# Modulation passes of a diffusion step's first layer: other places among the linear attention's VectorE work

## The chip, the cores and the metric

The kernel runs on one core of a Trainium2 chip. The metric is the device time of one launch in microseconds (us). The core's engines run side by side, each with its own queue of instructions in a fixed order: TensorE (PE in the profile, its weight loads PEld), VectorE (DVE), ScalarE (ACT), GpSimd (POOL) and SyncE (SP), whose queue issues nearly all DMA loads here. An instruction that waits holds up everything behind it on its engine.

## The reference, cut to what matters

A step of a diffusion backbone with two layers, over 512 latent and 128 context tokens of width 1024. Each layer has a mixer and a gated convolution FFN; both are modulated by vectors that come from a conditioning vector:

```python
def modulation(cvec, w, bias):
    mod = (jax.nn.silu(cvec) @ w + bias).reshape(-1, 1, 6 * D_MODEL)
    return jnp.split(mod, 6, axis=-1)      # sh1, sc1, g1, sh2, sc2, g2
...
hp = rms_norm(xp, norm_mix_g[i]) * (1.0 + sc1p) + sh1p
...
xp = xp + g1p * op
xp = xp + g2p * conv_ffn(rms_norm(xp, norm_ffn_g[i]) * (1.0 + sc2p) + sh2p, *ffn)
```

The same is done for the latent tokens with their own conditioning vector. The first layer's mixer is neighbourhood attention (8 heads) beside a bidirectional gated linear attention (4 heads, chunks, decay from log_sigmoid gates, forward and backward). The linear attention's gates are `log_sigmoid(lr @ w2 + b2) / 16`, summed along the tokens; its scores weigh q and k with exponentials of differences of these sums, its states carry k and v from tile to tile.

## The kernel before

All 640 tokens lie along the free axis, in two halves of 320; features lie on the partitions. Matmuls are done in three passes on a high and a low part (line 153): the weights are split into wh (ScalarE, line 111) and wl (VectorE or GpSimd, line 112).

**Modulation beside the first layer.** `modulations` is a generator. It makes three vectors (second gate of the mixer and the FFN's shift and scale) on VectorE, without TensorE: for each of 3 vectors, 8 feature tiles and 2 halves it loads a tile `wa` of 128x512 (256 KB, line 313, SP's queue, three buffers) and runs two scalar_tensor_tensor passes over it (line 316), one for the latent and one for the context vector, each with an accumulator read. That is one step; there are 48. Behind each vector's 16 steps come four small additions (lines 320 and 321).

**Order of the work.** The program's order is a priority: a planner gives each engine, at compile time, the ready instruction that stands first, by its own estimate of times. So an instruction may run well ahead of or behind its place in the program. `tc.issue_after(ins)` ties the instructions traced in its block to a place behind `ins` where they are on the same engine; instructions of other engines, and loads, aren't tied.

**The first layer.** `layer0` multiplies keys and queries of the linear attention, makes the low-rank input `lr` of the gates (weights `lrs`, lines 651 to 669), takes one step of the modulation, and then walks the linear attention: four gates (VectorE's `gmin`, line 730, ScalarE's exponentials and logarithms), four running sums `cum` (lines 743 and 745), then the pieces of `ORDER`: scores of m = 0 (`a0`), states of m = 0 (`s0`), scores of m = 1 (`a1`), output of m = 0 (`o0`), the first query projection (`q0`), `s1`, `o1`. m counts pairs of heads. Scores are made in six levels of growing block width and two off-diagonal ones: four subtractions on VectorE (`ea`, `eb`, lines 840 to 843), two exponentials on ScalarE, a product on GpSimd (line 846) and one on VectorE (line 847), small matmuls `lev` or `off` on TensorE, and a mask on VectorE (line 865). The tiles of this part share 16 buffers of one tag, `c`.

**Fill.** `Fill` holds generators of independent TensorE work (the products for v, the output gate rg, the attention's values: `tm` in lines 592 to 594 and `mm` in line 153) and hands out some of it at each call `fill.some(n)` along the chain: behind each gate, each sum, each level, in the states and in the outputs. `aside` holds the modulation. Its second argument `m` says how many modulation steps are taken at this call: SLEV = 2 at each of six levels, SOFF = 4 behind them, and 99, that is all that are left, ahead of the states.

Of the kernel before, what the change touches and what calls it, by code (L numbers as in the profile page):

```python
# [12 lines left out]
ALU = mybir.AluOpType  # L13
# [8 lines left out]
HN = NT // 2  # L22
# [8 lines left out]
def kernel(ctx: ExitStack, tc: tile.TileContext, a: dict, o: dict):  # L31
    nc = tc.nc
# [43 lines left out]
    def halves(t):  # L76
        return t[:, 0:NT].rearrange("p (h n) -> p h n", h=2)
# [29 lines left out]
    b2 = const("b2", [P, 2, 2])  # L107
# [131 lines left out]
    class Fill:  # L239


        def __init__(self):
            self.queue, self.aside, self.owed, self.after = [], [], 0.0, None

        def add(self, gen):
            self.queue.append(gen)
# [1 line left out]
        def first(self, gen):  # L248
            self.queue.insert(0, gen)

        def some(self, n, m=0):
            while m and self.aside:
                m -= 1
                if next(self.aside[0], self) is self:
                    self.aside.pop(0)
            self.owed += n
            n = int(self.owed)
            self.owed -= n
            while n and self.queue:
                with tc.high_priority(offset=0):  # L260
                    end = next(self.queue[0], self) is self
                if end:
                    self.queue.pop(0)
                else:
                    n -= 1

        def until(self, gen):

            while gen in self.queue:
                self.some(1)  # L270

        def all(self):
            while self.queue:
                self.some(1)


    mod = {}
# [353 lines left out]
    def layer0(H, raws):  # L631
        fill = Fill()
# [29 lines left out]
        ps = PS("lr")  # L662
# [52 lines left out]
        nxt = qk(0)  # L715
        barrier.clear()
        fill.aside.append(side)


        gscan = N("gscan")  # L720
# [4 lines left out]
        for m, d in keys:  # L725
            ps = PS("gate")
            for h in range(2):
                nc.tensor.matmul(ps[:, h, 0:HN], w2[:, d, 128 * m:128 * m + 128], lr[0:64, h * HN:(h + 1) * HN], start=True, stop=True)
            mn, ab = C("gmin"), C("gabs")
            nc.vector.tensor_scalar(halves(mn), ps[:, :, 0:HN], b2[:, d, m:m + 1], 0.0, ALU.add, ALU.min)  # L730
            nc.scalar.activation(halves(ab), ps[:, :, 0:HN], AF.Abs, bias=b2[:, d, m:m + 1])
            mins[m, d], logs[m, d] = mn, ab
            last = nc.scalar.activation(ab, ab, AF.Exp, scale=-1.0)
            fill.some(RG1)
# [3 lines left out]
        for key in keys:  # L738
            m, d = key
            nc.vector.tensor_tensor(mins[key], mins[key], logs[key], ALU.subtract)  # L740
            c = C("cum")
            if d == 0:
                nc.vector.tensor_tensor_scan(c, gscan, mins[key], 0.0, ALU.mult, ALU.add)
            else:
                nc.vector.tensor_tensor_scan(rev(c), gscan, rev(mins[key]), 0.0, ALU.mult, ALU.add)
            cum[key] = c
            fill.some(RG2)


        with tc.issue_after(last.ins):  # L750
            S, OT, att = {}, {}, {}

            def piece(kind, m):
                nonlocal last
                if kind == "a":
                    att.update(gla_scores(m, kg[m], qg[m], cum[m, 0], cum[m, 1], fill))
                elif kind == "s":
                    fill.until(g_vg)
                    fill.some(0, 99)
                    gla_states(m, kg[m], cum[m, 0], cum[m, 1], vg, S, fill)  # L760
                elif kind == "o":
                    last = gla_out(m, qg[m], cum[m, 0], cum[m, 1], vg, att, S, OT, fill)
                else:
                    fill.first(nxt)

            for p in ORDER:
                piece(p[0], int(p[1]))
        fill.until(g_va)
        with tc.issue_after(last):
            for t in rg:  # L770
# [52 lines left out]
    def rev(t):  # L823
        return t[:, ::-1]
# [7 lines left out]
    def gla_scores(m, k, q, F, G, fill):  # L832
        def level(h):

            ea, eb = C("ea"), C("eb")
            v = lambda t: t[:, 0:NT].rearrange("p (n s u) -> p n s u", s=2, u=h)
            n = NT // (2 * h)
            fm_ = v(F)[:, :, 0, h - 1:h].to_broadcast([P, n, h])
            gm_ = v(G)[:, :, 1, 0:1].to_broadcast([P, n, h])
            nc.vector.tensor_tensor(v(ea)[:, :, 0, :], fm_, v(F)[:, :, 0, :], ALU.subtract)  # L840
            nc.vector.tensor_tensor(v(ea)[:, :, 1, :], gm_, v(G)[:, :, 1, :], ALU.subtract)
            nc.vector.tensor_tensor(v(eb)[:, :, 0, :], v(G)[:, :, 0, :], gm_, ALU.subtract)
            nc.vector.tensor_tensor(v(eb)[:, :, 1, :], v(F)[:, :, 1, :], fm_, ALU.subtract)
            expo(ea[:, 0:NT], ea[:, 0:NT])
            expo(eb[:, 0:NT], eb[:, 0:NT])
            nc.gpsimd.tensor_tensor(ea[:, 0:NT], ea[:, 0:NT], k[:, 0:NT], ALU.mult)
            nc.vector.tensor_tensor(eb[:, 0:NT], eb[:, 0:NT], q[:, 0:NT], ALU.mult)  # L847
            return ea, eb

        accs = C("acc")  # L850
        acc, tmp = accs[:, 0:320], accs[:, 320:640]
        for li, h in enumerate(LEVELS):
            A, B = (k, q) if h == 0 else level(h)
            ps = PS("lev")
            for t in range(5):
                for e in range(2):
                    pe = slice(64 * e, 64 * e + 64)
                    for j in range(4):
                        s = slice(128 * t + 32 * j, 128 * t + 32 * j + 32)
                        nc.tensor.matmul(ps[32 * j:32 * j + 32, e, 32 * t:32 * t + 32], A[pe, s], B[pe, s], start=True, stop=True)  # L860
            for e in range(2):
                pv = ps[:, e, 0:160].rearrange("p (t i) -> p t i", i=32)
                mk = mask32[:, li:li + 1, :].to_broadcast([P, 5, 32])
                w = acc if li == 0 else tmp
                nc.vector.tensor_tensor(w[:, 160 * e:160 * e + 160].rearrange("p (t i) -> p t i", i=32), pv, mk, ALU.mult)
            if li:
                nc.gpsimd.tensor_tensor(acc[:, 0:320], acc[:, 0:320], tmp[:, 0:320], ALU.add)
            fill.some(RLEV, SLEV)
        A32, B32 = level(32)
        A64, B64 = level(64)  # L870
        fill.some(ROFF, SOFF)
        big, small = PS("off"), PS("offx")
        res = {}
        blocks = [(e, slice(64 * e, 64 * e + 64), t, big[:, e, 128 * t:128 * t + 128] if t < 4 else small[:, e, 0:128])
                  for e in range(2) for t in range(5)]
        for width in (32, 64):
            for e, pe, t, dst in blocks:
                if width == 32:
                    for j in range(4):
                        b = j // 2  # L880
                        s = slice(128 * t + 32 * j, 128 * t + 32 * j + 32)
                        nc.tensor.matmul(dst[32 * j:32 * j + 32, 64 * b:64 * b + 64], A32[pe, s],
                                         B32[pe, 128 * t + 64 * b:128 * t + 64 * b + 64], start=True, stop=True)
                    continue
                for b in range(2):
                    nc.tensor.matmul(dst[64 * b:64 * b + 64, 64 - 64 * b:128 - 64 * b],
                                     A64[pe, 128 * t + 64 * b:128 * t + 64 * b + 64],
                                     B64[pe, 128 * t + 64 - 64 * b:128 * t + 128 - 64 * b], start=True, stop=True)
        for e in range(2):
            x = C("att")  # L890
            nc.scalar.copy(x[:, 0:512], big[:, e, :])
            nc.scalar.copy(x[:, 512:640], small[:, e, 0:128])
            for j in range(4):
                pj = slice(32 * j, 32 * j + 32)
                nc.vector.tensor_copy(
                    x[pj, 0:NT].rearrange("p (t i) -> p t i", i=128)[:, :, 32 * j:32 * j + 32],
                    acc[pj, 160 * e:160 * e + 160].rearrange("p (t i) -> p t i", i=32),
                )
            res[m, e] = x
        return res  # L900

    def gla_states(m, k, F, G, vg, S, fill):
# [13 lines left out]
        for d in range(2):  # L916
# [13 lines left out]
            nc.sync.dma_start(s[:, 0, :], a["gla_s"][d, m])  # L930
            for i, t in enumerate(tiles[0:3]):
                nc.vector.scalar_tensor_tensor(s[:, i + 1, :], s[:, i, :], dec[d][:, t:t + 1], ds[:, 128 * i:128 * i + 128], ALU.mult, ALU.add)
            nc.vector.tensor_copy(s[:, 4, :], ds[:, 384:512])
            nc.gpsimd.dma_start(o["gla"][d, m], s[:, 4, :])
            S[m, d] = s
            fill.some(RST)
# [536 lines left out]
RLEV = 7  # L1473
ROFF = 12
RST = 8
ROUT = 6
SLEV = 2
SOFF = 4
ORDER = ("a0", "s0", "a1", "o0", "q0", "s1", "o1")
WPOOL = {'mix0': 2}  # L1480
NV = (False, True)
# [130 lines left out]
```

## Time and profile before

| | us |
|---|---|
| median of 3 runs | 1732.13 |
| lowest and highest run | 1729.12, 1733.19 |
| profiled execution, time | 1732.08 |
| profiled execution, span from first to last instruction | 1730.3 |
| VectorE busy over the span | 1280.7 (74%) |
| TensorE matmul busy over the span | 1640.0 (95%) |

The profile is of one execution. A row's busy time counts an instruction from its start to its end, with waits for a port inside it. Stretches are given in us from the start of the span.

### The profile page before, as it was taken

How to read it: one execution, taken by the hardware profiler on the slowest of the kernel's cores; microseconds unless marked ns; L12 is line 12 of the kernel's file. 1: busy time of each engine (PE TensorE's matmuls, PEld its weight loads, DVE VectorE, ACT ScalarE, POOL GpSimd, SP SyncE). 2: the span in 40 equal slices, each digit the busy share in tenths (PEclk: the TensorE clock that was granted, in tenths of full speed). 3: DMA queues.
4: the chain of work that ended last, by engine and by line, in shares of the span. 5: the costliest groups of instructions: out<-in, count | busy, mean ns of one | idle time of the engine just before them, and what ended most of it. 6: DMA issues, size and time to landing. Idle time of an engine off the chain costs nothing.

```text
span 1730.3 us, 33463 instructions
## 1 busy us (share of the span) xinstructions
PE 1640.0 (95%) x13142; PEld 1565.2 (90%) x13142; DVE 1280.7 (74%) x2877; ACT 720.9 (42%) x1599; POOL 206.5 (12%) x475
## 2 busy tenths in 40 slices
PE   7978798989999999999999999899999999999997
PEld 6867787878999999999998888789999999999997
DVE  5899955775899989996656987996776644663664
ACT  4443255453533313322335566665453322331342
POOL 2134441210200000000003310100100000000001
PEclk8988889999999999999998999999999999999998
DMA  8624323322255455444232200120222222222222
GB/s 317 204 86 133 108 90 97 101 88 92 81 165 164 152 165 183 151 149 128 70 122 87 68 20 13 42 63 20 80 66 82 74 74 73 74 69 91 72 66 71
DMA packets 68014, 175.22 MB, mean 101 GB/s; under 512 B 7920, under 2 KB 9744, under 8 KB 66832
## 3 DMA queue, kind: packets, MB, share of 16 engines
q1 hardware_dynamic: 67024, 171.48, 30.7%
q8 instruction: 103, 1.69, 0.4%
q0 software_dynamic: 832, 1.60, 0.3%
q14 instruction: 55, 0.45, 0.1%
HBM read 165.71 MB, written 7.34 MB: 100 GB/s over the span
## 4 chain that ended last, share of the span: by engine, by line
PE 78%; DVE 15%; DMA 3%; ACT 2%; issue 2%; SPq 0%; POOL 0%; ACTq 0%; DVEq 0%; POOLq 0%
PE mm L153 66%; DVE junk L316 2%; PE gpo L1297 2%; DVE wa L316 2%; PE gpt L1285 1%; DVE wl L112 1%; PE gs L1276 1%; DMA wa<-in_ada_wt_dram 1%; DVE mx L1023 1%; PE gs L1277 1%; PE napo L1089 1%; PE ss L410 1%; DVE eb L847 1%; DMA x<-in_xT_dram 0%; DVE q L613 0%
## 5 line engine op out<-in xcount | busy, mean ns | idle before, releaser
L153 PE MATMUL mm<-hh,wl 128*128 128x320 f32 x2080 | 652.6, 316 | 5.3 <-DVE x L488 1.9
L153 PE MATMUL mm<-hl,wh 128*128 128x320 f32 x2080 | 648.3, 312 | 0.6 <-DVE hl L456 0.6
L153 PE MATMUL mm<-hh,wh 128*128 128x320 f32 x2080 | 641.9, 312 | 0.0
L111 ACT CAST wh<-ws 128x512 fp32r<-128x512 f32 x376 | 228.8, 615 | 447.8 <-PE mm L153 420.5
L153 PEld LDWEIGHTS mm<-hh,wl 128*128 128x128 f32 x2080 | 394.5, 190 | 15.8 <-issue 5.5
L153 PEld LDWEIGHTS mm<-hl,wh 128*128 128x128 f32 x2080 | 395.2, 190 | 3.0 <-issue 1.2
L153 PEld LDWEIGHTS mm<-hh,wh 128*128 128x128 f32 x2080 | 393.4, 190 | 0.4
L112 DVE TENSOR_TENSOR wl<-ws,wh 128x512 fp32r<-128x512 f32 x348 | 242.2, 699 | 157.4 <-ACT wh L111 156.7
L153 PE MATMUL mm<-glo,wh 128*128 128x320 f32 x704 | 217.6, 310 | 0.0
L153 PE MATMUL mm<-ghi,wh 128*128 128x320 f32 x704 | 217.3, 310 | 0.0
L153 PE MATMUL mm<-ghi,wl 128*128 128x320 f32 x704 | 216.3, 310 | 0.0
L488 DVE SCALAR_TENSOR_TENSOR x<-mm,mod,x 128x192 f32<-128x192 f32 (+2 forms) x240 | 96.6, 435 | 84.1 <-PE mm L153 83.2
L153 PEld LDWEIGHTS mm<-ghi,wl 128*128 128x128 f32 x704 | 132.0, 188 | 0.9 <-issue 0.9
L153 PEld LDWEIGHTS mm<-glo,wh 128*128 128x128 f32 x704 | 132.6, 188 | 0.0
L153 PEld LDWEIGHTS mm<-ghi,wh 128*128 128x128 f32 x704 | 132.4, 188 | 0.1
L316 DVE SCALAR_TENSOR_TENSOR junk<-wa,sb 128x512 f32<-128x512 f32 x160 | 120.4, 757 | 9.4 <-DMA wa<-in_ada_wt_dram 7.0
L316 DVE SCALAR_TENSOR_TENSOR wa<-wa,sb 128x512 f32<-128x512 f32 x160 | 113.2, 714 | 0.2
L522 POOL MEMSET u<- 128x1 f32 x88 | 8.9, 102 | 767.2 <-DVE gate L515 432.5
L525 ACT COPY u<-mm 128x320 f32<-128x320 f32 x88 | 37.8, 431 | 87.6 <-PE mm L153 83.2
L1029 ACT ACTIVATE gp<-gs,mx,rq 128x640 f32<-128x640 f32 x64 | 56.9, 889 | 36.6 <-DVE mx L1025 27.9
L592 PE MATMUL tm<-wl,hh 128*128 128x256 f32 x200 | 61.3, 312 | 8.3 <-ACT v L601 4.0
L528 ACT COPY u<-mm 128x192 f32<-128x192 f32 x88 | 28.4, 322 | 78.8 <-PE mm L153 78.8
(302 smaller groups left out, 2452.7 us busy)
## 6 DMA issues: line engine op xcount, KB each, us to landing
ws<-in_wu_dram SPq DMA_DIRECT2D x88, 512.0 KB
wa<-in_ada_wt_dram SPq DMA_DIRECT2D x160, 256.0 KB
ws<-in_wd_dram SPq DMA_DIRECT2D x32, 448.0 KB
aw<-in_ada_w_dram SPq DMA_DIRECT2D x8, 1024.0 KB
ws<-in_w_ab_dram SPq DMA_DIRECT2D x16, 512.0 KB
ws<-in_wd_dram SPq DMA_DIRECT2D x16, 512.0 KB
x<-in_xT_dram SPq DMA_DIRECT2D x16, 320.0 KB
ws<-in_w_gqa_dram SPq DMA_DIRECT2D x10, 512.0 KB
```

The source lines that it names most:

```text
L111: nc.scalar.copy(hi, src)
L112: eng.tensor_tensor(lo, src, hi, ALU.subtract)
L153: nc.tensor.matmul(ps, x, y[:, s], start=st, stop=sp_)
L316: nc.vector.scalar_tensor_tensor(w if v else junk, w, 1.0, cs[v, j], ALU.mult, ALU.mult, accum_out=acc[:, k, v, j:j + 1])
L410: nc.tensor.matmul(ps[0:rows, c:c + 2], part[:, t], onesd, start=True, stop=True)
L488: nc.vector.scalar_tensor_tensor(x[:, b:e], ps[:, b - HN * h:e - HN * h], gate[:, v, m:m + 1], old[:, b:e], ALU.mult, ALU.add)
L525: nc.scalar.copy(u[:, 1:321], ps)
L528: nc.scalar.copy(u[:, 321:513], ps[:, 0:192])
L592: nc.tensor.matmul(ps, hh[:, s], wlo, start=(k == 0), stop=False)
L847: nc.vector.tensor_tensor(eb[:, 0:NT], eb[:, 0:NT], q[:, 0:NT], ALU.mult)
L1029: nc.scalar.activation(dst, src, AF.Exp, bias=mx[:, i:i + 1], accum_out=sm[:, i:i + 1], **kw)
L1297: last = nc.tensor.matmul(po[64 * f:64 * f + 64, 0:128], vs[t][:, 64 * kv:64 * kv + 64], mates[f]["x"][:, 128 * t:128 * t + 128], start=(t ...
```

## The change

Modulation steps are no longer the second argument of `some`. A new method `beside` takes steps, each tied behind `anchor`, the VectorE instruction that the chain last set. `some` adds `pace` (PACE = 3.0) to a counter at each call and takes as many steps; `queued` hands out the fill as before. The anchors are gmin, cum, the level's mask and the last copy of a state. Ahead of the states nothing is flushed any more; behind the last piece `beside(999)` would take what is left.

```diff
-        def some(self, n, m=0):
-            while m and self.aside:
-                m -= 1
-                if next(self.aside[0], self) is self:
-                    self.aside.pop(0)
+        def beside(self, n):
+
+            while n and self.aside:
+                n -= 1
+                with ExitStack() as behind:
+                    if self.anchor is not None:
+                        behind.enter_context(tc.issue_after(self.anchor.ins))
+                    if next(self.aside[0], self) is self:
+                        self.aside.pop(0)
+
+        def some(self, n):
+            self.due += self.pace
+            self.beside(int(self.due))
+            self.due -= int(self.due)
+            self.queued(n)
+
+        def queued(self, n):
             self.owed += n
...
         fill.aside.append(side)
+        fill.pace = PACE
...
-            nc.vector.tensor_scalar(halves(mn), ps[:, :, 0:HN], b2[:, d, m:m + 1], 0.0, ALU.add, ALU.min)
+            fill.anchor = nc.vector.tensor_scalar(halves(mn), ps[:, :, 0:HN], b2[:, d, m:m + 1], 0.0, ALU.add, ALU.min)
...
-                nc.vector.tensor_tensor_scan(c, gscan, mins[key], 0.0, ALU.mult, ALU.add)
+                fill.anchor = nc.vector.tensor_tensor_scan(c, gscan, mins[key], 0.0, ALU.mult, ALU.add)
...
-                    fill.some(0, 99)
...
+        fill.beside(999)
         fill.until(g_va)
...
-                nc.vector.tensor_tensor(w[:, 160 * e:160 * e + 160].rearrange("p (t i) -> p t i", i=32), pv, mk, ALU.mult)
+                fill.anchor = nc.vector.tensor_tensor(w[:, 160 * e:160 * e + 160].rearrange("p (t i) -> p t i", i=32), pv, mk, ALU.mult)
...
-            fill.some(RLEV, SLEV)
+            fill.some(RLEV)
...
-        fill.some(ROFF, SOFF)
+        fill.some(ROFF)
...
-            nc.vector.tensor_copy(s[:, 4, :], ds[:, 384:512])
+            fill.anchor = nc.vector.tensor_copy(s[:, 4, :], ds[:, 384:512])
...
-SLEV = 2
-SOFF = 4
+PACE = 3.0
```

The backward running sum (line 745) sets the anchor in the same way, and `until` and `all` call `queued` in place of `some`.

## Rows read from the trace of the kernel before

**Rows 1.** The page's 40 slices: busy tenths of TensorE and VectorE.
```profile
PE   7978798989999999999999999899999999999997
...
DVE  5899955775899989996656987996776644663664
```

**Rows 2.** Busy time by stretch: length, then per engine busy us and instructions, clock, DMA.
```profile
54.00:82.50 28.50, 25.86 (x162) 24.27 (x161) 26.61 (x68) 8.59 (x21) 5.60 (x4) 0.94 0.62 203
82.50:111.40 28.90, 25.86 (x256) 23.58 (x255) 28.01 (x61) 16.25 (x26) 4.11 (x2) 0.94 0.46 153
111.40:164.50 53.10, 38.88 (x708) 36.12 (x707) 53.10 (x104) 18.16 (x36) 26.12 (x16) 0.84 0.29 93
164.50:224.00 59.50, 47.75 (x777) 44.72 (x777) 59.37 (x128) 17.72 (x32) 27.80 (x19) 0.87 0.33 110
224.00:264.00 40.00, 39.37 (x426) 35.54 (x425) 17.75 (x35) 22.96 (x45) 17.34 (x15) 0.93 0.29 96
```

The engines' order is PE, PEld, DVE, ACT, POOL.

**Rows 3.** The same stretches, line 316 on VectorE alone.
```profile
54.00:82.50 28.50, 19.78 (x55) 0.94 0.62 203
82.50:111.40 28.90, 13.84 (x40) 0.94 0.46 153
111.40:164.50 53.10, 20.98 (x45) 0.84 0.29 93
164.50:224.00 59.50, 25.20 (x54) 0.87 0.33 110
```

**Rows 4.** TensorE's waits, 111.4 to 224 us, then 164.5 to 224: sum, times, longest.
```profile
PE lev L860 <- DVE eb L847: 14.2, 6, 5.2
...
PE ds L927 <- ACT kt L922: 2.7, 1, 2.7
...
PE lev L860 <- DVE eb L847: 7.5, 3, 4.9
```

**Rows 5.** VectorE's waits, 54 to 224 us.
```profile
DVE junk L316 <- DMA wa<-in_ada_wt_dram: 1.9, 5, 0.6
```

**Rows 6.** The chain of waits in 70 to 98 us: start, length, what; the longest of four DMA pieces.
```profile
82.01 4.15 DMA wa<-in_ada_wt_dram
```

**Rows 7.** SP's waits, 54 to 224 us.
```profile
SPq L313 <- DVE wa L316: 89.3, 39, 10.4
```

**Rows 8.** Timeline of ScalarE, VectorE and TensorE before the gates: start, length, instruction.
```profile
64.26 0.49 ACT L659 CAST lrs<-lrw 128x128 fp32r<-128x128 f32 x2
...
68.12 0.48 DVE L660 TENSOR_TENSOR lrs<-lrw,lrs 128x128 fp32r<-128x128 f32 x2
...
76.52 0.81 DVE L669 COPY lr<-lr 64x640 f32<-64x640 f32 x1
...
82.52 0.87 DVE L730 TENSOR_SCALAR gmin<-gate,b 128x640 f32<-128x640 f32 x1
...
62.28 0.44 PE L592 MATMUL tm<-wl,hh 128*128 128x256 f32 x1 [2.08 <-DVE wl L112]
...
75.29 0.46 PE L666 MATMUL lr<-hl,lrs 128*128 128x320 f32 x2
...
79.60 2.42 PE L728 MATMUL gate<-lr,w 64*128 64x320 f32 x8
```

**Rows 9.** TensorE busy behind 220 us: line 153, then line 592.
```profile
220.00:264.00 44.00, 15.57 (x92) 13.71 (x93) 0.89 0.28 94
...
220.00:264.00 44.00, 5.57 (x14) 4.20 (x14) 0.89 0.28 94
```

**Rows 10.** VectorE's groups of line 316, 164.5 to 224 us, then 54 to 82.5: busy, mean ns.
```profile
L316 DVE SCALAR_TENSOR_TENSOR junk<-wa,sb 128x512 f32<-128x512 f32 x13 | 13.1, 1021 | 0.0
L316 DVE SCALAR_TENSOR_TENSOR wa<-wa,sb 128x512 f32<-128x512 f32 x14 | 13.1, 938 | 0.0
...
L316 DVE SCALAR_TENSOR_TENSOR junk<-wa,sb 128x512 f32<-128x512 f32 x14 | 11.1, 791 | 3.4 <-DMA sb<-in_crow_dram 2.2 <-DMA wa<-in_ada_wt_dram 1.0
L316 DVE SCALAR_TENSOR_TENSOR wa<-wa,sb 128x512 f32<-128x512 f32 x14 | 9.3, 680 | 0.2
```

More of the change, by code (lines that the diff above doesn't have):

```diff
@@ L243, in __init__ @@
             self.queue, self.aside, self.owed, self.after = [], [], 0.0, None
+            self.pace, self.due, self.anchor = 0, 0.0, None
         def add(self, gen):
@@ L269, in until @@
             while gen in self.queue:
-                self.some(1)
+                self.queued(1)
         def all(self):
             while self.queue:
-                self.some(1)
+                self.queued(1)
     mod = {}
@@ L742, in layer0 @@
             if d == 0:
-                nc.vector.tensor_tensor_scan(c, gscan, mins[key], 0.0, ALU.mult, ALU.add)
+                fill.anchor = nc.vector.tensor_tensor_scan(c, gscan, mins[key], 0.0, ALU.mult, ALU.add)
             else:
-                nc.vector.tensor_tensor_scan(rev(c), gscan, rev(mins[key]), 0.0, ALU.mult, ALU.add)
+                fill.anchor = nc.vector.tensor_tensor_scan(rev(c), gscan, rev(mins[key]), 0.0, ALU.mult, ALU.add)
             cum[key] = c
```

## The prediction

> **What bounds the kernel now.** I read the page first. TensorE is busy 95% of the span, but that row is pipelined work with modelled ends, so it doesn't say where time can be won. The 40 slices do: slices 3 to 5 (86 to 216 us) are where TensorE drops to 7 or 8 tenths and VectorE stands at 9 [rows 1]. That is the linear attention of the first layer, the place of the change. Next come the busy times by stretch, cut where VectorE's work changes: 54 to 82.5 us (until the first gate result is read), 82.5 to 111.4 (gates and running sums), 111.4 to 164.5 (scores of m = 0), 164.5 to 224 (states of m = 0, scores of m = 1), 224 to 264 (the rest, before neighbourhood attention). VectorE is busy 26.6 of 28.5, 28.0 of 28.9, 53.1 of 53.1 and 59.4 of 59.5 us: a full engine for 170 us. Behind 224 it is busy 17.8 of 40 [rows 2]. Of the full stretch the modulation passes (line 316) take 19.8 + 13.8 + 21.0 + 25.2 = 79.8 us [rows 3]. One step is two passes over a 128x512 tile and two reads of an accumulator; 48 steps make 79.8 us, 1.66 us each.
>
> The list of waits says who suffers. TensorE waits in 111.4 to 224 us for VectorE's eb (14.2 us, six times, 7.5 us of it in the last stretch) and for ScalarE's kt (2.7) [rows 4]. VectorE itself waits only 1.9 us for the tiles wa [rows 5]. The chain of waits runs through VectorE from 54 to 220 us; in 70 to 98 us it holds four pieces, the longest 4.15 us, in which a step's load is what ends last [rows 6]. So the stage is bound by VectorE's throughput, and an order on a full engine wins nothing by itself: what counts is whether the engine has to idle anywhere, and whether TensorE has other work when this stage ends later.
>
> **What the change does.** It removes two steps per level, four behind the levels and the flush of all that are left ahead of the states; it adds three steps per call of the fill. The calls are: 4 behind the gates, 4 behind the running sums, 7 in the scores of m = 0, 2 in its states, then 15 more. One step is taken before. 47 steps and the closing additions are 48 calls of the generator, or 16 calls of the fill at three: 12 steps in the gates, 12 in the sums, 21 in the scores of m = 0, the last 2 and the closing additions in the first states. So "evenly over the linear attention" is its first half; m = 1 gets none. The tie holds VectorE's instructions alone: a step's load on SP's queue, its second part, isn't tied and stays bound by the three buffers of wa. SP waits 89.3 us for their release already, and loads of weights stand in line behind it [rows 7]; that stays. Nothing is put on ScalarE or GpSimd. What queues behind a tied step on VectorE: the next gate or sum, wl for the fill's weights, copies of v. Who waits for those: TensorE.
>
> **The sum.** It goes by the moment at which VectorE is through with the scores of m = 1 (224 us), against the profiled execution: span 1730.3, time 1732.08 us, so 1.8 lies around it; the median of the three runs is 1732.13, the same.
>
> 1. Steps lose their early place: +18.3. In 54 to 82.5 us 19.8 us of passes are done [rows 3], in time in which VectorE would otherwise wait for TensorE's products. Only the first step keeps its place, 1.5 us by its passes of 791 and 680 ns [rows 10]. 19.8 - 1.5 = 18.3 us go behind the first gate, into the full stretch.
>
> 2. The gates come earlier: -7.5. Without steps between, the weights lrs, whose last part is made at 68.12 us although its input is cast by 64.75, are ready 3.4 us earlier; TensorE's wait of 2.1 us for wl at 62.28 goes; the copy lr starts at 76.52 though the products end at 75.75 (0.8); the first gate result, whose two products out of eight (2.42 us) end by about 80.2, is read at 82.52 (2.3), behind passes; and the gate products start at 79.60 although lr is copied by 77.33 (2.3) [rows 8]. Together 10.9. They don't all add, since TensorE is busy 25.9 of the 28.5 us anyway [rows 2] and may do other products first. The certain ones (2.1 and 0.8) are 3, all are 11; I take 7.5, nearest to all but the 3.4 of lrs, as TensorE's products stand ahead of it.
>
> 3. Waits for wa: +1.5. No row shows 24 steps in a row tied to eight operations. In 70 to 98 us the loads are what ends last four times, with steps about as dense, and VectorE idled 1.9 us [rows 5, 6]. Bounds: 0 (three tiles lie ready and chain operations fill in) and +10: in 54 to 82.5 us 55 instructions, 13.75 steps, ran in 28.5 us, 2.07 us each [rows 3]; 24 steps at that instead of at 1.66 are 10 us more. I take 1.5, near the wait that the trace shows.
>
> 4. Waits beside GpSimd: -2. A pass over wa takes 938 ns on average in 164.5 to 224 us and 680 in 54 to 82.5; junk 1021 and 791 [rows 10]. GpSimd is busy 27.8 us in the former and 5.6 in the latter [rows 2]. The difference for the 27 passes of the last stretch is 13 x 0.230 + 14 x 0.258 = 6.6 us. With the steps gone from there, another VectorE operation may stand in their place and wait as long. Bounds -6.6 and 0; I take -2, nearer to 0, because VectorE is full in that stretch, so that something stands in the steps' place most of the time [rows 2]. The Trainium skill (SBUF — State Buffer, Who interferes with whom) says that a VectorE instruction with two SBUF inputs and a GpSimd instruction that reads SBUF hold a shared pair of ports each for its whole length, and the second blocks. The trace agrees in that the passes are longer where GpSimd is busy. By the rule the wait passes on to whichever VectorE instruction comes next: while the engine is full this term would be 0, and the sum +7.3.
>
> 5. Cover for TensorE: -5. If VectorE's stretch is longer, TensorE can do more of its fill inside it. Behind 220 us, 14 products of line 592 with their two partners are left of that fill, 5.6 us busy on line 592's row, overlapping with the partners', and 92 of line 153 (15.6 us) [rows 9]. The first can be drawn in; the second is the query projection, which needs the buffers that the scores of m = 1 hold. Bounds 0 and -18; I take -5.
>
> 6. Edits at no cost: the new method and counters are host code; the closing additions are the same; in the other stages the rate is given, but no steps are queued there. The modulation vectors are read from the output projection on, behind neighbourhood attention, and in program order all steps still stand ahead of the states of m = 1, so nobody waits for a vector; if that cover were gone, the last steps would cost their 1.66 us each.
>
> 18.3 - 7.5 + 1.5 - 2 - 5 = +5.3: 1732.1 + 5.3 = 1737.4 us. Ends: 18.3 - 11 + 0 - 6.6 - 18 = -17 and 18.3 - 3 + 10 = +25; all at one end at once is unlikely, half of that way is -7 and +15.
>
> **The rivals.**
>
> A, faster: the scores of m = 1 without steps. VectorE has them for itself, so that TensorE's waits of 7.5 for eb and 2.7 for kt in the last stretch [rows 4] go, while the longer gates cost TensorE nothing, because it has the products of v and of the gate rg for them (it is busy 25.9 of 28.9 us there now [rows 2]). At 8 of these 10.2 us won and nothing lost: 1724. It decides if the last mask of m = 1 ends before about 222 us. For it: TensorE's waits lie at the levels, not at the gates. Against it: the same VectorE work has to fit.
>
> B, no change: the fill covers the whole shift. TensorE is busy 39.4 of 40 us behind 224 [rows 2]; if all of term 5's 18 us can be drawn in, the end is bound by TensorE's own work: 1732, within 3.
>
> C, slower by more: loads bound the steps. If 24 steps in a row run at 2.07 us, the gates last 10 us longer, VectorE stands still behind a tied step whose tile hasn't landed, and SP's weights wait behind the loads: term 3 at its upper end, 1746.
>
> D, not as it says: the tie could change nothing where steps were already late. In the levels and after they run behind the chain's operations now (46.2 of 79.8 us lie there [rows 3]). But the 18 us ahead of the gates can't stay, so this is not likely; it would give 1732 and goes with B.
>
> **How the numbers follow.** Forecast 0.34 (1735.5 to 1744), A 0.28, B with D 0.25, C 0.13. The prediction is 1737.4. A measurement of this kernel can tell about 0.2% (3.5 us) from no change. The range has to leave out at most 2 in 10: from 1722 (A's 1724, less 2) to 1749 (C's 1746, plus 3). Faster by over 0.2%: A, 0.28. Within: B and D, and little of the forecast's lower edge, 0.25. Slower by over 0.2%: 0.34 + 0.13 = 0.47. The forecast's own range is 1733 to 1744.
>
> **What the new profile would show.** Term 1: about 1.5 us of line 316 ahead of the first gate result, 24 steps in gates and sums, none in the scores of m = 1. Term 2: the first read of a gate at 72 to 79 us instead of 82.5. Term 3: VectorE's wait for wa at 1 to 4 us; at 10, C. Term 4: passes at 700 to 800 ns on average, and the levels' own operations in m = 1 no slower than now. Term 5: few products of line 592 behind the scores of m = 1. The last running sum, at 111.4 us now, should end at about 124 (75 plus 12 gate and sum operations of 14 us plus 24 steps at 1.5), and the scores of m = 1 at 225 to 235. If they end at 224 or before, terms 1 and 2 are wrong; if they end at 232 and the time is the same, term 5 is.

## The result, and the profile after

The changed kernel takes 1742.68 us (median of four runs, 1739.03 to 1744.38), the kernel before 1731.74 beside it (1729.12 to 1733.19). The ratio is 1.0057, 95% interval 1.0033 to 1.0080: slower by 10.9 us between the medians, where +5.3 was forecast. The profiled executions, on which the working below rests, differ by 12.3 us (spans 1742.6 and 1730.3).

Lines of the stage have moved by 13 or 14: the passes are line 329 now (316 before), their loads 326 (313), the gate's first read 744 (730), the running sums 757 and 759, the product eb 861 (847), the first score of neighbourhood attention 1072 (1058).

The page's slices of TensorE and VectorE first, as in [rows 1]:

```profile
PE   7978779989999999999999999999999999999997
...
DVE  5699975766899999997656898897776644663654
```

Counted from 1, as in the prediction, slice 2 (44 to 87 us) has lost some of its VectorE work, 6 tenths where it had 8, and slice 6 (218 to 261 us) has TensorE at 7 where it had 9. By stretch, cut near the same events as [rows 2] (first gate read, last running sum, end of the scores of m = 0, of m = 1, first score of neighbourhood attention; the cut at 241 lies 3 us behind the last product eb of m = 1, the one at 224 in the kernel before 3 us ahead of it); after the length stand PE, PEld, DVE, ACT and POOL, then the clock and the DMA:

```profile
54.00:75.80 21.80, 21.50 (x146) 20.77 (x145) 9.27 (x17) 8.81 (x21) 5.71 (x6) 1.00 0.43 149
75.80:105.50 29.70, 26.26 (x253) 23.24 (x253) 28.27 (x57) 16.51 (x26) 4.20 (x3) 0.94 0.42 133
105.50:165.00 59.50, 47.18 (x749) 44.15 (x748) 57.02 (x112) 19.54 (x37) 25.71 (x17) 0.86 0.30 99
165.00:241.00 76.00, 59.50 (x932) 53.77 (x932) 71.92 (x164) 20.96 (x39) 30.24 (x21) 0.86 0.37 120
241.00:280.00 39.00, 30.26 (x256) 27.69 (x255) 22.75 (x50) 21.10 (x39) 16.52 (x14) 0.83 0.30 102
```

The passes alone, line 329 on VectorE, against [rows 3]:

```profile
54.00:75.80 21.80, 1.40 (x4) 1.00 0.43 149
75.80:105.50 29.70, 13.13 (x40) 0.94 0.42 133
105.50:165.00 59.50, 26.47 (x53) 0.86 0.30 99
165.00:241.00 76.00, 36.63 (x87) 0.86 0.37 120
241.00:280.00 39.00, 4.54 (x11) 0.83 0.30 102
```

Ahead of the first gate 19.78 us of passes have become 1.40. Gates and sums hold as many as before, 10 steps and not 24. What was displaced has gone behind them: 5.5 us more in the scores of m = 0, and 36.63 + 4.54 us behind 165 us, where the kernel before had 25.20. No stretch is free of steps.

VectorE's waits in 50 to 240 us (sum, times, longest), against [rows 5], then SP's, against [rows 7]:

```profile
DVE junk L329 <- DMA wa<-in_ada_wt_dram: 9.3, 10, 1.9
DVE lr L682 <- PE lr L679: 5.5, 1, 5.5
DVE wl L112 <- ACT wh L111: 3.6, 2, 2.9
```

```profile
SPq L326 <- DVE wa L329: 91.5, 37, 15.2
```

The wait for wa is 9.3 instead of 1.9 us; the waits for lr and wl lie in the time ahead of the gates, in which VectorE had passes to do before. Four events from the timelines of the changed kernel (start, length, instruction), then the last two of them in the kernel before:

```profile
75.82 0.88 DVE L744 TENSOR_SCALAR gmin<-gate,b 128x640 f32<-128x640 f32 x1 [2.62 <-PE gate L742]
...
104.09 1.46 DVE L759 TENSOR_TENSOR_SCAN cum<-gscan,gmin 128x640 f32<-128x640 f32 x1
...
237.29 0.81 DVE L861 TENSOR_TENSOR eb<-eb,kqg 128x640 f32<-128x640 f32 x1
...
280.16 0.39 PE L1072 MATMUL nas<-kk,q 128*128 128x256 f32 x1
```

```profile
226.18 0.81 DVE L847 TENSOR_TENSOR eb<-eb,kqg 128x640 f32<-128x640 f32 x1
...
266.25 0.35 PE L1058 MATMUL nas<-kk,q 128*128 128x256 f32 x1 [1.47 <-ACT kk L698]
```

The first gate is read 6.7 us earlier, the last product eb of m = 1 starts 11.1 us later, the first score of neighbourhood attention 13.9 us later. What follows that score is nearly the same in both: 1742.6 - 280.2 = 1462.4 us, and 1730.3 - 266.3 = 1464.0. So the whole difference arises ahead of 280 us, and from here on a run is read at the start of these two, the marks **last eb** and **first score**. The marks don't give the time alone: in five of the runs below what follows the first score is 4.6 to 6.7 us longer or shorter than in the kernel before.

**Where the 11.1 us up to last eb come from.** From the first gate's read to the end of last eb the kernel before takes 144.5 us, the changed one 162.3: 17.8 more. VectorE's passes in between are 60.0 and 74.3 us (+14.3), its other work 83.0 and 81.0 (-2.1), its idle time 1.5 and 7.0 (+5.5, the waits for wa). 14.3 - 2.1 + 5.5 = 17.8, less the 6.7 by which the gates come earlier: 11.1.

### The profile page after: what moved, and what is told of

Read it like the earlier page. It is cut to its first block, busy times and chain, and to the rows that moved or that the text cites. A ratio compares the mean times of both kernels' runs of the same rounds, so it can differ in the third digit from the quotient of the medians.

```text
span 1742.6 us, 33451 instructions
## 1 busy us (share of the span) xinstructions
PE 1649.5 (95%) x13142; PEld 1572.5 (90%) x13142; DVE 1283.0 (74%) x2877; ACT 722.0 (41%) x1599; POOL 206.2 (12%) x475
## 4 chain that ended last, share of the span: by engine, by line
PE 78%; DVE 14%; DMA 4%; ACT 2%; issue 2%; SPq 0%; POOL 0%; ACTq 0%; DVEq 0%; POOLq 0%
PE mm L153 66%; DMA wa<-in_ada_wt_dram 2%; DVE junk L329 2%; PE gpo L1311 2%; DVE wa L329 2%; PE gpt L1299 1%; DVE wl L112 1%; PE gs L1290 1%; PE napo L1103 1%; DVE mx L1037 1%; PE gs L1291 1%; PE ss L423 1%; DVE eb L861 1%; DMA x<-in_xT_dram 1%; DVE gp L1051 1%
## 5 line engine op out<-in xcount | busy, mean ns | idle before, releaser
L329 DVE SCALAR_TENSOR_TENSOR wa<-wa,sb 128x512 f32<-128x512 f32 x160 | 117.2, 738 | 0.2
```

Source lines behind the costliest of these rows:

```text
L329: nc.vector.scalar_tensor_tensor(w if v else junk, w, 1.0, cs[v, j], ALU.mult, ALU.mult, accum_out=acc[:, k, v, j:j + 1])
```

## The experiments

Three theories stood at first. T: the tie keeps passes out of the time ahead of the gates, in which VectorE idles, and the engine has to make up for them later. P: the steps' places in program order are the cost. L: the steps' loads are, which three buffers let through one by one. Later runs ask a second question, what late steps cost; its theories (S, Q, D, R) are told in the expectations.

### The tie taken away

```diff
-                    if self.anchor is not None:
-                        behind.enter_context(tc.issue_after(self.anchor.ins))
```

> The changed kernel without the tie: steps stand at the same places in the program, three per call, but may run ahead of them. Theory T (the tie keeps 12 steps out of the time ahead of the gates, and VectorE has to make up for them): about 19 us of line 329's passes lie ahead of the first gate result again, the last product eb of the scores of m = 1 ends at 225 to 229 us instead of 238.1, and the time falls by 8 to 13 us to 1730 to 1735, about that of the kernel before. Rival P (the cost comes from the places in the program, with three steps ahead of each following operation of the chain): the steps are still in the way of gates and sums, and the time stays at 1739 to 1745.

1733.26 us, ratio 1.0013 (1.0000 to 1.0026). The passes in two stretches, and the first score:

```profile
50.00:75.00 25.00, 14.78 (x39) 0.93 0.73 247
75.00:112.00 37.00, 19.62 (x56) 0.95 0.45 145
```

```profile
265.14 0.36 PE L1070 MATMUL nas<-kk,q 128*128 128x256 f32 x1 [1.47 <-ACT kk L709]
```

The passes are back ahead of the gates (1.40 with the tie), the first score is back at 265. Three steps per call without the tie cost 0.13%, with an interval that begins at nothing, against 0.57% with it. T held, P fell: the places can be only a small part of the cost.

### Thirteen steps untied, the rest tied

```diff
-        next(side)
+        for _ in range(13):
+            next(side)
...
-PACE = 3.0
+PACE = 2.25
```

> The changed kernel with 13 steps instead of 1 taken untied ahead of the gates, and the other 35 tied as in the change at 2.25 per call, so that they end at the same place. Theory T: 18 us of passes go back ahead of the gates, which start 4 to 7 us later; the last product eb of m = 1 ends 8 to 12 us earlier than 238.1, time 1730 to 1735. Rival P: the ties and places within the gates and sums cost, not the early time; 1738 to 1743. Rival L (loads bound the steps): the loads come as late as before, VectorE's waits for wa stay at 9 us, and no more than half of the 11 us comes back, 1736 to 1740.

1735.45 us, ratio 1.0030 (1.0020 to 1.0040). 12.86 us of passes in 50 to 75 us, last eb at 227.98, but first score at 271.82; VectorE waits 6.3 us for wa. About half of the loss is back, between T's and L's numbers. Up to last eb nearly all is back (1.8 us behind the kernel before); the rest arises behind it, in 43.8 us from last eb to first score against 40.1. The trace shows what stands there: the off products that use last eb start 9.7 us behind it instead of 5.9, since TensorE has 41 products of the fill (`tm`) left between the two marks where it had 26. TensorE's timeline:

```profile
237.64 0.69 PE L901 MATMUL off<-eb,ea 64*64 64x64 f32 x18
```

### All but three of the loads left out

The tie and the three steps per call stay; the steps multiply three tiles that lie there, again and again.

```diff
-                    w = T("wa", "wa", n=512, bufs=NWA)
-                    nc.sync.dma_start(w, a["ada_wt"][n, k, :, 512 * j:512 * j + 512])
+                    if len(todo) == 3 and len(kept) == 3:
+                        w = kept[(2 * k + j) % 3]
+                    else:
+                        w = T("wa", "wa", n=512, bufs=NWA)
+                        nc.sync.dma_start(w, a["ada_wt"][n, k, :, 512 * j:512 * j + 512])
+                        kept.append(w)
```

> The changed kernel with the loads of the first layer's modulation left out, all but three: the passes run over the same three tiles again (the modulation vectors are left uncomputed by that). Theory T: the early place is the larger cost and stays, VectorE's waits for wa of 9.3 us go; steps run where they are tied, 24 in gates and sums, none in the scores of m = 1, so that the last running sum ends at 115 to 125 us instead of 105.5; the last product eb of m = 1 ends 5 to 9 us earlier than 238.1; time 1733 to 1738. Rival L (the loads are the whole cost): time at or below the kernel before, 1725 to 1732. Rival N (loads don't matter): within 3 us of the change, 1740 to 1746.

1735.80 us, ratio 1.0030 (1.0018 to 1.0042), first score at 272.30. VectorE's waits in 50 to 240 us:

```profile
...
DVE junk L333 <- DMA wa<-in_ada_wt_dram: 1.1, 1, 1.1
```

Of the wait for wa 1.1 us are left, last eb comes at 232.32 instead of 237.29 and the first score 7.9 us earlier. So about half of what the tie costs runs through the loads: a step that could have run in idle time now runs where the loads, too, must keep pace. It isn't pure, since the run also takes the steps' traffic off SP and the DMA engines. The rest, 6 us up to last eb, is work that VectorE has to do later, loads or not: from the first gate's read to the end of last eb it is busy 157.6 of 158.0 us. T's picture of the steps was wrong in one point: with no load to wait for, they still ran until 239 us and the last sum still ended at 105. So the loads aren't the main reason why the steps run late; that the planner's order puts the chain's operations ahead of the steps is my reading.

### The tie on the places of the kernel before

```diff
-        def some(self, n):
-            self.due += self.pace
-            self.beside(int(self.due))
-            self.due -= int(self.due)
+        def some(self, n, m=0):
+            self.beside(m)
...
+                    fill.some(0, 99)
                     gla_states(m, kg[m], cum[m, 0], cum[m, 1], vg, S, fill)
```

(The levels take SLEV = 2 and the off products SOFF = 4 again.)

> The tie alone, on the places of the kernel before: two steps behind each level, four behind the last, the flush ahead of the states of m = 0. No step can now run ahead of the first level, at about 100 us: the passes of the gates and sums (13 us more than in the change) go behind too. T (what counts is how much of the passes is done before the running sums end; VectorE makes up the rest behind them): 1.5 us of passes ahead of the last sum, which ends at 92 to 100; the first score of neighbourhood attention at 284 to 294, and 1747 to 1757. P (the tie costs only together with three steps per call): first score at 264 to 272, 1730 to 1738.

1758.73 us, ratio 1.0166 (1.0153 to 1.0179), a little above T's upper end. Gates and sums by stretch, all engines, then the passes alone, then the first score:

```profile
75.00:98.00 23.00, 21.09 (x223) 18.33 (x223) 14.66 (x15) 15.88 (x26) 3.77 (x2) 1.00 0.09 28
```

```profile
75.00:98.00 23.00, 0.00 (x0) 1.00 0.09 28
```

```profile
292.44 0.55 PE L1071 MATMUL nas<-kk,q 128*128 128x256 f32 x1 [11.28 <-DVE kk L711]
```

With the first tied step behind the first level no pass runs in 75 to 98 us, VectorE stands idle for 8 of 23 us, and the last sum ends at 98 instead of 105. Last eb is early, 223.58, because more than a third of the passes (30.5 us) is still to come then; they put the first score at 292. The tie alone, on the old places, costs more than the tie on the new ones: three steps per call *soften* the tie, since they offer steps from the first gate on.

### The rate without the tie

```diff
-                    if self.anchor is not None:
-                        behind.enter_context(tc.issue_after(self.anchor.ins))
...
-PACE = 3.0
+PACE = 2.2
```

> The change without the tie and with 2.2 steps per call instead of 3, between the two other untied runs: the steps' last calls are in the scores of m = 1. T: passes ahead of the gates as in the kernel before (13 to 15 us ahead of the first), first score of neighbourhood attention 263 to 267, 1728 to 1734: without the tie the rate doesn't matter. Q: a late step or two ahead of q, first score at 268 to 274, 1734 to 1741.

1731.20 us, ratio 1.0005 (0.9995 to 1.0015), first score 264.34: T's numbers. At 1.6, without the tie:

> The change with two edits: no tie, and 1.6 steps per call of the fill instead of 3, so that the calls reach to the last output of m = 1. Against the run with the tie at 1.6 (1756) it tells what the tie adds, against the untied run at 3 (1733) what the late calls add. T (the tie is the cost, places are not): passes ahead of the first gate at 13 to 15 us, first score of neighbourhood attention at 262 to 268, 1728 to 1735. Q (late places cost by themselves, through steps ahead of q on VectorE's queue): passes ahead of the gate as before, but the first score at 270 to 282, 1737 to 1748.

1735.25 us, ratio 1.0027 (1.0016 to 1.0039). Neither picture: the first score comes at 265.05, as T said, and the time is that which Q gave. Six passes run at 238 to 249 us, behind last eb; what follows the first score takes 1735.8 - 265.1 = 1470.7 us, 6.7 more than in the kernel before. VectorE's wait for a load of the bias of neighbourhood attention, which ends at 282 us, is 4.5 us and was 1.4: about half of the delay arises on SP, one stage later, and the rest wasn't traced.

### The same rate with the tie

```diff
-PACE = 3.0
+PACE = 1.6
```

> The changed kernel with 1.6 steps per call instead of 3: 38 of the 47 steps stand ahead of the end of the scores of m = 1 in the program, the rest in the outputs. Theory T (VectorE is full until the scores of m = 1 are done, and only steps that run before that cost): nine steps of 1.66 us leave the full stretch, the last product eb of m = 1 ends 8 to 14 us earlier than 238.1, and the time is 1728 to 1736. Rival L (steps run as late as their loads let them, whatever the pace): steps, products and the time stay as with the change, within 3 us, 1740 to 1746.

1756.21 us, ratio 1.0149 (1.0130 to 1.0168); both theories missed. Last eb comes at 227.28, 10 us earlier than at three steps per call, as T said, and the first score at 291.81. VectorE's timeline, then SP's:

```profile
268.90 0.69 DVE L329 SCALAR_TENSOR_TENSOR wa<-wa,sb 128x512 f32<-128x512 f32 x1
...
277.56 0.69 DVE L329 SCALAR_TENSOR_TENSOR junk<-wa,sb 128x512 f32<-128x512 f32 x1 [7.97 <-DMA wa<-in_ada_wt_dram]
...
279.54 0.69 DVE L112 TENSOR_TENSOR wl<-ws,wh 128x512 fp32r<-128x512 f32 x1
280.25 1.67 DVE L626 TENSOR_TENSOR q<-qx,q 64x640 fp32r<-64x640 f32 x2
```

```profile
248.47 10.12 SPq L795 DMA_DIRECT2D vw<-values  x5
261.23 1.21 SPq L326 DMA_DIRECT2D wa<-in_ada_wt_dram  x2
262.52 1.74 SPq L795 DMA_DIRECT2D vw<-values  x3
264.36 2.64 SPq L326 DMA_DIRECT2D wa<-in_ada_wt_dram  x1
```

The last step's load is issued at 264 us, behind eight loads of the values of neighbourhood attention; VectorE stands for 8 us in front of it, and the weights wl and the queries q of the first scores stand behind it on VectorE. This is why the first score is the second mark: a late step can cost its load's place on SP, here 8 us, and not its 1.66 us.

### The last steps moved behind the scores, untied

The next five start from the kernel before and take the flush apart; they ask whether rival A's gain, scores of m = 1 without steps, can be had. First the flush behind the last output of m = 1:

```diff
-                    fill.some(0, 99)
                     gla_states(m, kg[m], cum[m, 0], cum[m, 1], vg, S, fill)
...
                 piece(p[0], int(p[1]))
+        fill.some(0, 99)
```

> The kernel before, with one edit: the flush of all steps that are left, ahead of the states of m = 0, is put behind the last output of m = 1. So 16 steps go to each of the two score stages and the rest come behind the linear attention. Two theories. S (the stage: VectorE's work ahead of the last mask of m = 1 sets the end): some ten steps, 16 us of passes, leave the stage; the last product eb of m = 1 ends at 210 to 218 us instead of 227, the first score of neighbourhood attention starts at 255 to 262 instead of 266, and the time is 1720 to 1728. Q (the queue: neighbourhood attention starts when VectorE has made q and kk of the query projection, and steps that stand ahead of them on its queue delay that, with the waits for their loads): eb ends as early, but the first score starts at 270 to 290, and the time is 1735 to 1755.

1753.68 us, ratio 1.0138 (1.0122 to 1.0153): last eb where S had it, 211.63, and the time where Q had it. Busy times of 164.5 to 224 us, against the fourth row of [rows 2], and the first score:

```profile
164.50:224.00 59.50, 56.83 (x924) 51.12 (x923) 40.17 (x68) 19.39 (x35) 28.95 (x22) 0.90 0.18 59
```

```profile
281.11 0.55 PE L1058 MATMUL nas<-kk,q 128*128 128x256 f32 x1 [4.85 <-ACT kk L698]
```

Without a pass there, TensorE is busy 56.8 of 59.5 us where it was 47.8: 9 us of its waits are gone, and rival A's mechanism is real. But the passes come at 230 to 284 us, one of them waits 11.4 us for its load, and kk waits behind it.

About seven steps late, behind the query projection of the first heads:

```diff
-                    fill.some(0, 99)
+                    fill.some(0, 0 if m else 8)
...
+            fill.some(0, 99)
             xs, proj = [], OutProjection(a["w_abo"], 4, mod[0, 2])
```

> The kernel before with other places for its last steps: the flush ahead of the states of m = 0 takes 8 steps instead of all, none are taken ahead of the states of m = 1, and the rest come behind the query projection of the first heads, ahead of the output projection's set-up. No tie. About seven steps, 14 passes, leave the scores of m = 1 and stand behind the first kk on VectorE. S (the stage sets the end, and late steps are free where nothing of the chain stands behind them): last eb of m = 1 at 213 to 220 us instead of 227, first score of neighbourhood attention at 255 to 263 instead of 266, 1720 to 1728. Q (late steps and their loads cost what the stage wins): eb as early, but the steps' loads stand on SP between the values of neighbourhood attention and its bias, the first score at 262 to 275 or the bias of the first scores late by 4 us or more, 1731 to 1745.

1737.94 us, ratio 1.0031 (1.0019 to 1.0044). Last eb at 215.39, 11 us early; q is made at 243 us. Then VectorE's timeline and SP's:

```profile
272.65 0.69 DVE L316 SCALAR_TENSOR_TENSOR junk<-wa,sb 128x512 f32<-128x512 f32 x1 [15.81 <-DMA wa<-in_ada_wt_dram]
```

```profile
243.92 14.98 SPq L781 DMA_DIRECT2D vw<-values  x8
259.00 2.38 SPq L783 DMA_DIRECT2D vc<-in_na_vc_dram  x1
261.48 14.06 SPq L313 DMA_DIRECT2D wa<-in_ada_wt_dram  x4
```

The fourth late step finds its tile not yet asked for: SP is at the values for 15 us, and turns to the steps' loads 4.6 us after VectorE has begun to stand. VectorE stands 15.8 us, with weights wl and the second half of kk behind it, the first score comes at 276.81, and the 11 us are gone. With the last 16 steps there:

> As the run with about seven late steps, but with no flush ahead of the states of m = 0 at all: 16 steps in each of the two score stages by program, and the last 16 behind the query projection of the first heads. No tie. Some 15 steps, 30 passes, run behind the first kk, part of them among the first scores of neighbourhood attention. S: last eb at 210 to 214, first score at 252 to 262, 1717 to 1727. Q: the first score at 262 to 275, and the later scores wait for the steps: about 15 steps of 1.5 us, 22 us, of which VectorE has 17 of 36 us free in 264 to 300; 1735 to 1755.

1743.70 us, ratio 1.0064 (1.0047 to 1.0082), Q's time again: last eb 214.29, one wait of 14.7 us, first score at 276.78.

So the late steps were split, four behind the last output of m = 1, the rest behind the query projection, so that the loads of the latter are issued ahead of the values:

```diff
                 piece(p[0], int(p[1]))
+        fill.some(0, 4)
```

> As the run with about seven late steps, but four of these stand behind the last output of m = 1 and three behind the query projection of the first heads, so that the loads of the last three are issued on SP ahead of the values of neighbourhood attention, in the time in which VectorE idles behind the last mask of m = 1. No tie. D (what put the gain back there was the one wait of 15.8 us for a load issued behind the values): last eb again at 213 to 217 us, no wait of VectorE for a load above 3 us, first score of neighbourhood attention at 256 to 263, 1720 to 1729. R (late steps cost by themselves, as work ahead of q and kk on VectorE): eb as early, first score at 264 to 272, 1730 to 1738.

1731.28 us, ratio 1.0005 (0.9993 to 1.0018): no difference, where D had 1720 to 1729. The cause that D named is confirmed by its marks, the gain isn't there. In the profiled execution VectorE has no wait for wa left behind last eb (those ahead of it, 5.2 us, have 2.3 as the longest), last eb comes at 216.60 and the first score at 261.45, 4.8 us ahead of the kernel before, and the span is 1725.2. But that execution (1727.0 us) is the fastest of eleven, which reach to 1736.5; what spreads the others wasn't found. With the loads of all steps also set higher in the order:

```diff
-                    nc.sync.dma_start(w, a["ada_wt"][n, k, :, 512 * j:512 * j + 512])
+                    with tc.high_priority(offset=EVAC):
+                        nc.sync.dma_start(w, a["ada_wt"][n, k, :, 512 * j:512 * j + 512])
```

> The same with the loads of all steps set higher in the order, so that SP issues each as soon as its tile is free by the plan, ahead of other loads of the same time. D: the scores of m = 1 hold no step, last eb at 212 to 216, first score at 254 to 262, 1718 to 1728. R: first score at 264 to 272, 1730 to 1738, and the weights that now stand behind the loads on SP may come later in the gates: first gate read later than 82.5 us by 1 to 3.

1734.94 us, ratio 1.0026 (1.0012 to 1.0040); last eb at 222.90, first score at 268.70, R's numbers. D's condition wasn't met: 13.9 us of passes still run in 164.5 to 224 us.

The traces show a second reason why an early last eb buys little, beside the late loads. The kernel before has 26 products of the fill between last eb and the first score; the kernels whose flush takes eight steps have 52 or 53. In the split kernel last eb is 9.6 us earlier than in the kernel before, the off products behind it (225.30 instead of 232.06) 6.8 and the first score 4.8. No kernel of this study beats the kernel before.

## Why the prediction was right or wrong

**Direction and range held, the size was half.** +5.3 was forecast, +10.9 measured between the medians. The sum goes by the end of the scores of m = 1, which it puts at 224 us; the trace has last eb at 226.18, ending at 227.0. Up to there the first four terms forecast +10.3 and 11.1 was measured. That near hit is luck, for misses of 4 to 6 us cancel in it. What made the size half is term 5. Term by term, at the profiled executions:

- *Term 1, steps lose their early place, +18.3:* right, 19.80 - 1.40 = 18.4. What the prediction didn't see is where they go: not into gates and sums, so that m = 1 is free, but into both score stages and behind them. 6.5 us of passes run behind last eb, which takes 6.5 off the mark and puts them ahead of the copies of att. The step that failed in the mechanism is "21 in the scores of m = 0, the last 2 and the closing additions in the first states": it counted calls of the fill as if steps ran where they are called. They run where the tie, the order of the instructions and the loads let them, which is later.
- *Term 2, gates earlier, -7.5:* right, -6.7 (75.82 instead of 82.52).
- *Term 3, waits for wa, +1.5:* mis-sized. VectorE's waits rose from 1.9 to 9.3 us, +5.5 of it between first gate and last eb. I took the value near the wait that the trace of before showed [rows 5], but there the loads had 28.5 us ahead of the gates in which 13.75 steps ran [rows 3], and now they have to let the same 48 steps through in the time that is left. The chain of waits had spoken against it: four of its pieces in 70 to 98 us were loads [rows 6], the buffers were already what SP waited for most [rows 7]. Rival C had the mechanism, at 0.13, and the run without loads shows its share, 1.0030 instead of 1.0057. But C put the waits into the gates, where 1.1 us of them lie: gates and sums take 29.7 us instead of 28.9.
- *Term 4, passes faster away from GpSimd, -2:* wrong in sign. All passes together take 79.8 us before and 82.2 after, since they still run beside GpSimd. The rule of the Trainium skill that was weighed there (SBUF — State Buffer, Who interferes with whom) made it 0 while VectorE is full, which is nearer.
- *Term 5, cover for TensorE, -5:* mis-sized, and the reason why the size was half: +1.2 was measured (+2.8 up to the first score, -1.6 behind it). The bound of -18 doesn't follow from the 5.6 and 15.6 us that it names. The cover itself came. In the kernel before the off products that use last eb stand behind 26 products of the fill on TensorE and start 5.9 us behind it; in the changed kernel no such product is left, and they start 1.0 us behind it. But the chain then goes on through VectorE, to the copies of att, and there the late passes and their loads take the 4.9 us back. ScalarE's parts of att are ready at 240.9 us, VectorE's copies come at 246.21. TensorE and VectorE in the kernel before, then in the changed one:

```profile
232.06 0.69 PE L886 MATMUL off<-eb,ea 64*64 64x64 f32 x18
...
234.60 2.58 DVE L895 COPY att<-acc 32x160 f32<-32x160 f32 x8 [3.01 <-ACT att L892]
...
247.56 1.38 PE L952 MATMUL go<-att,v 128*128 128x128 f32 x10 [0.64 <-ACT got L959]
```

```profile
238.25 0.69 PE L900 MATMUL off<-eb,ea 64*64 64x64 f32 x18 [0.77 <-DVE eb L861]
...
246.21 1.92 DVE L909 COPY att<-acc 32x160 f32<-32x160 f32 x6
...
260.71 2.51 PE L966 MATMUL go<-att,v 128*128 128x128 f32 x10 [5.29 <-ACT got L973]
```

From last eb to the first score it was 40.1 us before, TensorE busy for 38.0 of them, and is 42.9 now, TensorE busy for 32.3. TensorE also pays for its idling: it stands for 5.3 us up to 260.7, the granted clock of 257 to 263 us is 0.50, the lower of its two levels (1.2 GHz), and ten products `go` take 2.51 us where they took 1.38 at a clock of 1.00. What that costs in all wasn't measured apart; the mean granted clock between the two marks is 0.96 before, 0.84 in the changed kernel and 0.74 to 0.79 in the three slowest runs, so part of the cost of late steps in them may be clock.

18.4 - 6.5 - 6.7 + 5.5 + 2.4 - 2.0 (other work of VectorE that left the stretch) = 11.1 up to last eb, +2.8 from there to the first score, -1.6 behind it: +12.3 in the profiled executions.

**The rivals.** A (1724) didn't happen, because m = 1 didn't become free of steps; where it was made so, the stage won 9 us of TensorE's waits, about the 8 that A named, and late loads and the fill behind last eb took them. B and D (1732) fell: the cover is worth 4.9 us at the off products and not the whole shift, and the late passes took it back; the tie changes much (1.0057 with it, 1.0013 without). Of "what the new profile would show", the passes ahead of the first gate (1.40) and the gate's first read (75.82) came as said; the last sum (105.5 instead of about 124), the passes' mean (892 and 860 ns instead of 700 to 800) and the scores' end (238 instead of 225 to 235) didn't.

**What is open.** How the half that the loads cost divides between the wait for buffers and the traffic that the run without loads also took away; why TensorE draws less of its fill ahead of last eb with thirteen early steps; what the lower clock behind late steps costs; and the spread of the split kernel.

## What to carry to other kernels

Background work that a full engine has to do is cheapest in the holes that the engine has anyway, so tying it behind the chain's operations loses exactly the holes that lie ahead of the chain; ask first where the engine idles, and let the work run there. Whoever moves work with its own loads should follow the loads in their queue first: an instruction in order on an engine waits for a load that is in order behind something else, and all that stands behind it waits too (15.8 us here, for work of 1.4). And a cover has to be judged at the event that the next stage starts from, here the first score of neighbourhood attention, not by how much work TensorE has drawn ahead.

## What the runs showed of the hardware

A pass over a 128x512 tile mostly takes 0.68 us (the mean of the second passes in 54 to 82.5 us, [rows 10]), and up to three times as long beside GpSimd's multiplications of 128x640 tiles. In the split kernel, four passes in a row from 233.65 us took 2.0 us each while GpSimd ran four such multiplications, which themselves took 1.9 to 2.0 us each instead of the 1.5 of the two ahead of them. VectorE's timeline, then GpSimd's:

```profile
233.04 0.68 DVE L316 SCALAR_TENSOR_TENSOR junk<-wa,sb 128x512 f32<-128x512 f32 x1
...
233.65 2.04 DVE L316 SCALAR_TENSOR_TENSOR junk<-wa,sb 128x512 f32<-128x512 f32 x1
...
235.62 2.02 DVE L316 SCALAR_TENSOR_TENSOR wa<-wa,sb 128x512 f32<-128x512 f32 x1
...
237.57 2.04 DVE L316 SCALAR_TENSOR_TENSOR junk<-wa,sb 128x512 f32<-128x512 f32 x1
...
239.54 2.03 DVE L316 SCALAR_TENSOR_TENSOR wa<-wa,sb 128x512 f32<-128x512 f32 x1
```

```profile
228.63 3.06 POOL L945 TENSOR_TENSOR qd<-qd,kqg 128x640 f32<-128x640 f32 x2 [2.79 <-ACT qd L832]
...
233.23 3.86 POOL L914 TENSOR_TENSOR kd<-kd,kqg 128x640 f32<-128x640 f32 x2 [1.53 <-ACT kd L832]
237.05 3.97 POOL L945 TENSOR_TENSOR qd<-qd,kqg 128x640 f32<-128x640 f32 x2
```

So both engines lost, and steps put into VectorE's idle time there cost 2.0 us a pass rather than 0.7. The trace agrees with the Trainium skill (SBUF — State Buffer, Who interferes with whom) that such instructions of the two engines take turns at a shared port: a pass lasts about as long as the multiplication beside it. One after the other the two would take 0.68 + 1.53 = 2.2 us; from the start of one pass to the next it is 1.96.
